# A pre-norm's turn from tokens to channels: rows scaled on VectorE and transposed on TensorE, in place of float32 products with a diagonal matrix

## The chip, the core and the metric

The kernel runs on one core of a Trainium2 chip. The metric is the device time of one execution in microseconds (us), and the changed kernel is compared with the kernel before it on the same chip. Matrix products are done by TensorE (PE in the profile; PEld is its weight load), elementwise work by VectorE (DVE) and ScalarE (ACT), and nearly all weights are loaded by DMAs that SyncE (SP) issues.

## What is computed

A two-layer encoder on 256 tokens of 2048 channels, in float32. Every sub-layer f is, with the shift, scale and gate of an adaLN projection of a conditioning vector c:

```python
x = x + gate * RMSNorm_post(f(RMSNorm_pre(x) * (1 + scale) + shift))

def _rms(x):
    x32 = x.astype(jnp.float32)
    return x32 * lax.rsqrt(jnp.mean(jnp.square(x32), axis=-1, keepdims=True) + EPS)
```

The sub-layers are a convolution module and a gated feed-forward network (layer 0), then gated linear attention and a gated feed-forward network (layer 1). So there are four pre-norms. The change concerns the turn of RMSNorm_pre(x) from rows of tokens to rows of channels, which the products that follow need.

## The kernel before

The residual stream stays on the chip as eight tiles `X[t][c]`: two halves `t` of 128 tokens on the partitions, and four pieces `c` of 512 channels along them. Weights come in blocks of 1 MB (`raw`, DMAs at L95). ScalarE casts a block to a float32r part `hi` (L119), VectorE subtracts to get the rest `lo` (L121), and each product with a weight is done as three float32r products (L751 to L753 in the convolution's first projection `ps_cin`, L406 and L407 in the networks' `ps_fa` and `ps_fb`). The adaLN weights ride along: as rows on VectorE (L348, 128 x 2048) or as columns on TensorE (`ada`, L362), whose sums VectorE turns (`adat`, L369) and TensorE adds (`adas`, L376).

A pre-norm works in three steps. `token_rstd` makes 1/rms of 128 tokens, one number per partition. `token_diag` puts it on the diagonal of a 128 x 128 matrix `dg` (L464). `h_tiles` then takes two blocks of 128 channels at a time and makes, for both halves of the tokens, the product of the block of `X` with `dg` (L474, tile `ps_h`): the product scales the rows and transposes them at once. One `ps_h` tile holds two blocks, so four products. ScalarE writes the modulated norm `h` (L481) and for odd blocks its unrounded copy `hn` (L483), VectorE does `hn` for even blocks (L485) and the part below float32r (L486). In names like `ps_h00_4` the digits are the layer, the norm and the first of the two blocks.

In the convolution's pre-norm the sixteen blocks are made in five steps (blocks 0-1, 2-3, 4-7, 8-11, 12-15), each just behind the adaLN columns of its own scale and shift, between the products of the first projection. The other three pre-norms stand behind a post-norm: `post_norm` adds the sub-layer's output `y` to `X` (L561), sums its squares on ScalarE (L425), keeps TensorE busy meanwhile with products that are not used (`clock`, L549), and calls `token_diag`. There all sixteen blocks follow each other.

Each engine works through its own instructions strictly in the order of a schedule that is made when the program is built; a scheduler lays them out by its own estimates, so a change in one function can move the instructions of others. Temporary tiles come from small pools: `adat`, squares and a few others share three buffers (`sq`).

Of the kernel before, what the change touches and what calls it, by code (L numbers as in the profile page):

```python
# [24 lines left out]
# blocks of channels whose convolution is done on the tensor engine  # L25
PE_BLOCKS = (5, 7, 9, 11, 12, 13, 14, 15)
# blocks whose mean the squares are taken around
NA = 12
# steps of the first projection: input tiles, and the pairs of channels and gates that they meet
STEPS = ((0, 2, 0, 16), (2, 2, 0, 16), (4, 4, 0, 16), (8, 4, 0, 8), (12, 4, 0, 8), (8, 8, 8, 16))  # L30
# adaLN blocks that are loaded after every block of weights of a step
ADA = ((2, 1, 1, 0), (3, 3, 2, 0), (1, 1, 1, 1, 1, 1, 1, 1), (3, 3, 2, 0), (1,) * 4, (1,) * 8)
COLS_CONV = 16
# the heads' steps: a head's waits lie beside the next head's products
# [14 lines left out]
# columns of the packed per-channel parameters  # L49
# [13 lines left out]
class Stream:  # L63
    """Weight blocks in the order they are used: loaded ahead, split into two
    float32r parts ahead of the products; adaLN weights ride along."""

    def __init__(self, tc, ctx, items, ada_row, ada_col, raw_bufs=4, split_bufs=4):
# [15 lines left out]
        # blocks whose parts are kept in another pool  # L83
# [42 lines left out]
    def flush(self):  # L126
        """adaLN products come after the arithmetic that was waiting already."""
        self.finish()
        for it, r in self.late:
            (self.ada_row if it["kind"] == "row" else self.ada_col)(it["key"], r)  # L130
        self.late.clear()

    def finish(self):
        """The sums of products that were taken out of PSUM before."""
        for f in self.sums:
            f()
        self.sums.clear()
# [17 lines left out]
    def prepare(self, n, first=SPLIT_FIRST):  # L155
        """Split the next n blocks."""
        self.first = first
        i = self.pos
        for _ in range(n):
            i = self._next(i) + 1  # L160
        self.run_to(i)
# [15 lines left out]
class Later(list):  # L177
    """Tiles that are made, two at a time, as the first products come to them."""
# [10 lines left out]
def trunk_kernel(ctx: ExitStack, tc: tile.TileContext, x, cvec, ccol, adar, adac, adah, par, taps, wgate,  # L189
# [21 lines left out]
    # per tile of 128 inputs: silu(c) in the first of 32 columns  # L211
# [8 lines left out]
    # channel n of 32 on every partition (i, n)  # L220
# [4 lines left out]
    # the residual stream, tokens on partitions  # L225
# [28 lines left out]
    def ada_step(s):  # L254
        """The adaLN blocks of a step's scale and shift."""
# [89 lines left out]
    def ada_row(key, r):  # L345
        """128 outputs of an adaLN product, rows of the transposed weights."""
# [4 lines left out]
    def ada_col(key, r):  # L351
        """512 outputs of an adaLN product on the tensor engine: four column tiles
        take four input tiles at once, and a product with ones sums their rows."""
# [10 lines left out]
        if i == KT // per - 1:  # L364
            # output 128 c + 32 a + i: four partial sums, on partitions (j, i) of column 32 (4 c + a)
# [29 lines left out]
    pp = {"ps": ctx.enter_context(tc.tile_pool(name="psum", bufs=6, space=PS))}  # L395

    def mm_blocks(keys, act, nk=KT):
        """Columns of 128-wide weight blocks against act (parts hi | lo): PSUM
        [:, :T] + [:, T:] is the product. Several blocks go through the input tiles together."""
# [22 lines left out]
    def token_squares(src, ss, t, c):  # L422
        """The sum of squares of every token over 512 channels."""
# [13 lines left out]
    def warm(func, src):  # L437
        """Brings in a function's table while its data is still on the way."""
# [9 lines left out]
    def add_bias(l, m):  # L448
        """Row products lack their bias; column products have it."""
# [10 lines left out]
    def token_diag(ss, name):  # L460
        """1 / rms of 128 tokens, on the diagonal of a matrix."""
        r = token_rstd(ss, name)
        dg = small.tile([P, P], F32, tag="dgx", name="dgx" + name, bufs=2)
        apool["dg"] = V.tensor_scalar_mul(dg, ident, r)  # L464
        return dg

    def h_tiles(l, which, sh, sc, dg, ks):
        """Channels of the modulated norm: the product with the diagonal scales and transposes."""
        hs = []
        for k0 in ks[::2]:  # L470
            ps = pp["ps"].tile([P, 2, T], F32, tag="ps", name=f"ps_h{l}{which}_{k0}")
            for k in (k0, k0 + 1):
                for t in range(2):
                    nc.tensor.matmul(ps[:, k - k0, t * P : (t + 1) * P], X[t][k // 4][:, (k % 4) * P : (k % 4 + 1) * P],  # L474
                                     dg[t], start=True, stop=True)
# [24 lines left out]
    def gate_rows(l, which, gate, room=None):  # L500
        """gate * norm_g along the channels, the same on every partition."""
# [12 lines left out]
    def token_products(pv, t, parts, act, kt, nk):  # L514
        """A tile of inputs: 512 output channels of half of the tokens."""
# [8 lines left out]
    def mm_tokens(key, act, nk, each, last=False):  # L524
        """512 output channels, tokens on partitions, all the parts summed in PSUM.
        Last: one half of the tokens after the other, so that the first's norm runs
        beside the second's products."""
# [17 lines left out]
    def keep_clock(src, tag="ada"):  # L545
        """Products without a use: the array's clock falls when it waits for long."""
# [4 lines left out]
    def post_norm(l, which, t, ss, ys, last=False):  # L551
        """x += y / rms(y), y with its gains; the sums of squares of the new x."""
# [15 lines left out]
        return None if last else token_diag(sx[t], f"x{l}{which}{t}")  # L568
# [22 lines left out]

    def conv_mixer(l):
        with early as cx:
# [8 lines left out]
            dg = [token_diag(ss[t], f"in{t}") for t in range(2)]  # L602
# [30 lines left out]
            def mean_add(j):  # L633
                """The statistics of the channels: sums, and the squares of the
                distances from the mean of the first NA blocks."""
# [12 lines left out]
            def tap(j, s):  # L648
                """The weights of the channels of a block, s steps back."""
# [3 lines left out]
            def gather(j, ps, last):  # L653
                """The sums over the steps of the inputs of a pair: channels and their gate."""
# [18 lines left out]
            def taps_dve():  # L673
                """The taps of two blocks in turns."""
# [455 lines left out]
```

## The time and the profile before

| | us |
|---|---|
| median of 3 runs | 2391.42 |
| lowest, highest | 2387.24, 2392.43 |
| span of the profiled execution | 2389.3 |
| PE busy in it | 2332.2 |
| DVE busy in it | 1775.8 |
| ACT busy in it | 1226.6 |

The profiled execution is shown with its span from the first to the last instruction; no separate device time is listed for it, and the span lies 2.1 us under the median. Busy time counts an engine's instructions as they lie on the clock, so overlapping ones are counted once. The profile counts each float32 product of `h_tiles` as two matmuls with two weight loads: 256 records for 128 products.

### The profile page before, as it was taken

How to read it: one execution, taken by the hardware profiler on the slowest of the kernel's cores; microseconds unless marked ns; L12 is line 12 of the kernel's file. 1: busy time of each engine (PE TensorE's matmuls, PEld its weight loads, DVE VectorE, ACT ScalarE, POOL GpSimd, SP SyncE). 2: the span in 40 equal slices, each digit the busy share in tenths (PEclk: the TensorE clock that was granted, in tenths of full speed). 3: DMA queues.
4: the chain of work that ended last, by engine and by line, in shares of the span. 5: the costliest groups of instructions: out<-in, count | busy, mean ns of one | idle time of the engine just before them, and what ended most of it. 6: DMA issues, size and time to landing. Idle time of an engine off the chain costs nothing.

```text
span 2389.3 us, 34229 instructions
## 1 busy us (share of the span) xinstructions
PE 2332.2 (98%) x13522; PEld 1952.7 (82%) x13522; DVE 1775.8 (74%) x2522; ACT 1226.6 (51%) x1941; POOL 17.4 (1%) x43
## 2 busy tenths in 40 slices
PE   6999998999999999999999999999999999999998
PEld 5888746788878888888878888887888888888886
DVE  3878998788878888778878876756887466655665
ACT  5334465465534554345565576656554455534543
POOL 0000000000000000000000000000000000000000
PEclk9999998999999999999999999999999999999999
DMA  9877768657799778988947756563777655555553
GB/s 385 363 311 292 303 230 306 258 211 274 291 326 358 286 283 317 365 282 299 339 154 268 282 203 217 176 228 107 290 273 262 214 180 191 185 190 191 192 198 119
DMA packets 86578, 609.31 MB, mean 255 GB/s; under 512 B 10064, under 2 KB 10128, under 8 KB 13456
## 3 DMA queue, kind: packets, MB, share of 16 engines
q1 hardware_dynamic: 84800, 601.84, 68.5%
q0 software_dynamic: 1472, 4.23, 0.6%
q8 instruction: 106, 1.74, 0.3%
q10 hardware_dynamic: 144, 1.05, 0.1%
q14 instruction: 56, 0.46, 0.1%
HBM read 604.94 MB, written 2.13 MB: 254 GB/s over the span
## 4 chain that ended last, share of the span: by engine, by line
PE 94%; DMA 2%; DVE 1%; ACT 1%; issue 0%; SPq 0%; DVEq 0%; ACTq 0%
PE ps_fa L406 13%; PE ps_fb L406 13%; PE ps_fb L407 7%; PE ps_fa L407 7%; PE ps_fo L522 6%; PE ps_fo L521 6%; PE ps_fo L520 6%; PE ps_cin L751 3%; PE ps_cin L752 3%; PE ps_cin L753 3%; PE ps_r L406 3%; PE ada L362 2%; PE ps_r L407 1%; PE ps_cout L520 1%; PE ps_k L406 1%; PE ps_cout L522 1%
## 5 line engine op out<-in xcount | busy, mean ns | idle before, releaser
L121 DVE TENSOR_TENSOR lo<-raw,hi 128x1024 fp32r<-128x1024 f32 (+1 forms) x760 | 914.7, 1214 | 415.3 <-ACT hi L119 412.0
L119 ACT CAST hi<-raw 128x1024 fp32r<-128x1024 f32 (+1 forms) x760 | 784.5, 1042 | 838.3 <-PE ps_fa L406 196.0
L406 PE MATMUL ps_fa<-h,hi 128*128 128x512 f32 x1408 | 501.0, 398 | 0.9 <-ACT h L481 0.9
L406 PE MATMUL ps_fb<-h,hi 128*128 128x512 f32 x1408 | 500.8, 397 | 0.0
L407 PE MATMUL ps_fa<-h,lo 128*128 128x256 f32 x1408 | 394.5, 280 | 1.7 <-DVE lo L121 1.7
L407 PE MATMUL ps_fb<-h,lo 128*128 128x256 f32 x1408 | 394.5, 280 | 1.5 <-DVE lo L121 1.5
L348 DVE CUSTOM_DVE_ANT_0 raw<-raw,cb 128x2048 f32<-128x2048 f32 x140 | 319.8, 2286 | 18.9 <-DMA raw<-in_adar 18.5
L406 PEld LDWEIGHTS ps_fa<-h,hi 128*128 128x128 f32 x1408 | 264.4, 188 | 64.8 <-issue 1.2
L406 PEld LDWEIGHTS ps_fb<-h,hi 128*128 128x128 f32 x1408 | 264.4, 188 | 64.6
L521 PE MATMUL ps_fo<-lo,u 128*128 128x512 f32 x704 | 274.1, 389 | 1.3 <-DVE lo L121 1.3
L522 PE MATMUL ps_fo<-hi,u 128*128 128x512 f32 x704 | 273.9, 389 | 0.0
L520 PE MATMUL ps_fo<-hi,u 128*128 128x512 f32 x704 | 272.8, 389 | 0.0
L407 PEld LDWEIGHTS ps_fa<-h,lo 128*128 128x128 f32 x1408 | 265.7, 189 | 2.8 <-DVE lo L121 2.1
L407 PEld LDWEIGHTS ps_fb<-h,lo 128*128 128x128 f32 x1408 | 265.7, 189 | 1.8 <-DVE lo L121 1.8
L521 PEld LDWEIGHTS ps_fo<-lo,u 128*128 128x128 f32 x704 | 132.2, 188 | 29.4 <-DVE lo L121 2.1
L520 PEld LDWEIGHTS ps_fo<-hi,u 128*128 128x128 f32 x704 | 132.2, 188 | 27.5 <-ACT hi L119 0.2
L522 PEld LDWEIGHTS ps_fo<-hi,u 128*128 128x128 f32 x704 | 132.2, 188 | 27.4
L751 PE MATMUL ps_cin<-h,hi 128*128 128x256 f32 x512 | 147.6, 292 | 6.1 <-ACT hi L119 6.0
L753 PE MATMUL ps_cin<-h,lo 128*128 128x256 f32 x512 | 144.5, 287 | 2.3 <-DVE lo L121 2.3
L752 PE MATMUL ps_cin<-h,hi 128*128 128x256 f32 x512 | 146.2, 288 | 0.4 <-DVE h L486 0.4
L751 PEld LDWEIGHTS ps_cin<-h,hi 128*128 128x128 f32 x512 | 99.6, 196 | 18.3 <-ACT hi L119 8.5
L752 PEld LDWEIGHTS ps_cin<-h,hi 128*128 128x128 f32 x512 | 99.9, 196 | 5.6 <-DVE h L486 4.7
(239 smaller groups left out, 2884.7 us busy)
## 6 DMA issues: line engine op xcount, KB each, us to landing
raw<-in_fin SPq DMA_DIRECT2D x176, 1024.0 KB, 4.8
raw<-in_adar SPq DMA_DIRECT2D x140, 1024.0 KB, 6.1
raw<-in_fout SPq DMA_DIRECT2D x88, 1024.0 KB, 5.0
raw<-in_adac SPq DMA_DIRECT2D x44, 1024.0 KB, 5.5
raw<-in_gin SPq DMA_DIRECT2D x33, 1024.0 KB, 5.7
raw<-in_cin SPq DMA_DIRECT2D x32, 1024.0 KB, 11.3
raw<-in_cout SPq DMA_DIRECT2D x16, 1024.0 KB, 7.0
raw<-in_gv SPq DMA_DIRECT2D x16, 1024.0 KB, 4.8
```

What stands on the lines that cost most here:

```text
L119: nc.scalar.copy(hi[:, :w], r[:, s : s + w])
L121: nc.vector.tensor_sub(lo[:, :w], r[:, s : s + w], hi[:, :w].bitcast(F32))
L348: V.tensor_tensor_reduce(out=r, in0=r, in1=cb, scale=1.0, scalar=0.0, op0=ALU.mult, op1=ALU.add, accum_out=mod[l, m][:, k : k + 1])
L362: nc.tensor.matmul(ps[32 * (j % 4) : 32 * (j % 4) + 32], cz[:, kt], r[:, j * n : (j + 1) * n], start=kt < 4, stop=kt >= KT - 4, tile_posit ...
L406: nc.tensor.matmul(ps, hi(k * P), act[k], start=k == 0, stop=False)
L407: nc.tensor.matmul(ps[:, :T], lo(k * P), act[k][:, :T], start=False, stop=k == nk - 1)
L520: nc.tensor.matmul(pv, ah, wh, start=kt == 0, stop=False)
L521: nc.tensor.matmul(pv, ah, wl, start=False, stop=False)
L522: nc.tensor.matmul(pv, al, wh, start=False, stop=kt == nk - 1)
L751: nc.tensor.matmul(ps[:, b], hi(o), ah, start=k == 0, stop=False)
L752: nc.tensor.matmul(ps[:, b], hi(o), al, start=False, stop=False)
L753: nc.tensor.matmul(ps[:, b], lo(o), ah, start=False, stop=k == nk - 1)
```

## The change

`token_diag` becomes `token_normed`: VectorE multiplies the four 128 x 512 pieces of `X[t]` with 1/rms, into the tiles of the post-norm's `y`, which are no longer needed by then. `h_tiles` transposes the scaled blocks on TensorE. In the convolution's pre-norm, which has no `y` tiles, a function `normed` scales two blocks of one half of the tokens (128 x 256) when they are asked for, into a tile `xs` of the pool's tag `sq`. Line numbers behind these places grow by 1 or 11. Comments and docstrings are dropped too, which changes no instruction.

```diff
-    def token_diag(ss, name):
-        """1 / rms of 128 tokens, on the diagonal of a matrix."""
+    def token_normed(t, ss, xs, name):
         r = token_rstd(ss, name)
-        dg = small.tile([P, P], F32, tag="dgx", name="dgx" + name, bufs=2)
-        apool["dg"] = V.tensor_scalar_mul(dg, ident, r)
-        return dg
+        for c in range(4):
+            i = V.tensor_scalar_mul(xs[c], X[t][c], r)
+            if c == 0:
+                apool["dg"] = i
+        return lambda k: xs[k // 4][:, (k % 4) * P : (k % 4 + 1) * P]
...
                 for t in range(2):
-                    nc.tensor.matmul(ps[:, k - k0, t * P : (t + 1) * P], X[t][k // 4][:, (k % 4) * P : (k % 4 + 1) * P],
-                                     dg[t], start=True, stop=True)
+                    nc.tensor.transpose(ps[:, k - k0, t * P : (t + 1) * P], dg[t](k), ident)
...
-        return None if last else token_diag(sx[t], f"x{l}{which}{t}")
+        return None if last else token_normed(t, sx[t], [ys[t, c] for c in range(4)], f"x{l}{which}{t}")
...
-            dg = [token_diag(ss[t], f"in{t}") for t in range(2)]
+            rs = [token_rstd(ss[t], f"in{t}") for t in range(2)]
+            two = {}
+
+            def normed(t, k):
+
+                if k % 2 == 0:
+                    two[t] = small.tile([P, 2 * P], F32, tag="sq", name=f"xs{t}{k}", bufs=3)
+                    V.tensor_scalar_mul(two[t], X[t][k // 4][:, (k % 4) * P : (k % 4 + 2) * P], rs[t])
+                return two[t][:, k % 2 * P : (k % 2 + 1) * P]
+
+            dg = [lambda k, t=t: normed(t, k) for t in range(2)]
```

The built program has 128 matmuls and 128 weight loads fewer on TensorE, and 32 more multiplications on VectorE. The schedule moves with it, above all in the convolution's first projection. Three places follow, each of before and then of the changed kernel. A row gives the line, the operation, out<-in and the shape.

**Place 1, the step of blocks 4-7.** TensorE before; `ps_cin1_12` is the next product of the projection.

```order
L362 MATMUL ada014_700<-raw21_630,cz_80 32x512 x4
L474 MATMUL ps_h00_4_889<-dgxin0_168,x01_93 128x128
L474 MATMUL ps_h00_4_889<-dgxin1_174,x11_97 128x128
...
L376 MATMUL adas014_877<-adat0140_862,mask32_88 32x2 x4
...
L376 MATMUL adas014_877<-adat014256_864,mask32_88 32x2 x4
L474 MATMUL ps_h00_6_904<-dgxin1_174,x11_97 128x128
L751 MATMUL ps_cin1_12_919<-h00_2_558,hi23_0_794 128x256
```

TensorE in the changed kernel, at the same place:

```order
L362 MATMUL ada014_704<-raw21_634,cz_80 32x512 x4
L376 MATMUL adas014_881<-adat0140_866,mask32_88 32x2 x4
L376 MATMUL adas014_881<-adat014256_868,mask32_88 32x2 x4
L476 MATMUL ps_h00_4_893<-ident_85,xs04_894 128x128
L476 MATMUL ps_h00_4_893<-ident_85,xs14_897 128x128
...
L476 MATMUL ps_h00_6_912<-ident_85,xs06_913 128x128
L762 MATMUL ps_cin1_12_931<-h00_2_562,hi23_0_798 128x256
```

The products with `dg` stood ahead of and between the `adas`; the transposes stand behind both, five of them ahead of the projection's next product. VectorE in the changed kernel there:

```order
L369 STREAM_TRANSPOSE adat0140_866<-ada014_704 128x256
L369 STREAM_TRANSPOSE adat014256_868<-ada014_704 128x256
L121 TENSOR_TENSOR lo23_0_799<-raw23_638,hi23_0_798 128x1024
L121 TENSOR_TENSOR lo23_1024_803<-raw23_638,hi23_1024_802 128x1024
L379 TENSOR_TENSOR m01_101<-adas014_881,pr_84 128x4
L624 TENSOR_TENSOR m00_100<-m00_100,pr_84 128x4
L610 TENSOR_SCALAR xs04_894<-x01_93,trin0_164 128x256
L458 SCALAR_TENSOR_TENSOR m01_101<-m01_101,pr_84 128x4
L610 TENSOR_SCALAR xs14_897<-x11_97,trin1_168 128x256
L610 TENSOR_SCALAR xs06_913<-x01_93,trin0_164 128x256
```

The rows down to L624 stood there before in the same order; the three scalings came in behind them.

**Place 2, the step of blocks 8-11.** VectorE before:

```order
L660 TENSOR_TENSOR pair13_596<-pair13_596,ps_cin2_13_1413 128x512
L348 ISA raw39_1179,m00_100<-raw39_1179,cb_83 128x2048
...
L369 STREAM_TRANSPOSE adat0180_1443<-ada018_1039 128x256
L369 STREAM_TRANSPOSE adat018256_1445<-ada018_1039 128x256
L121 TENSOR_TENSOR lo40_0_1452<-raw40_1242,hi40_0_1451 128x1024
L121 TENSOR_TENSOR lo40_1024_1456<-raw40_1242,hi40_1024_1455 128x1024
```

VectorE in the changed kernel:

```order
L348 ISA raw39_1191,m00_100<-raw39_1191,cb_83 128x2048
...
L671 TENSOR_TENSOR pair13_600<-pair13_600,ps_cin2_13_1425 128x512
L624 TENSOR_TENSOR m00_100<-m00_100,pr_84 128x4
L369 STREAM_TRANSPOSE adat0180_1455<-ada018_1051 128x256
L121 TENSOR_TENSOR lo40_0_1464<-raw40_1254,hi40_0_1463 128x1024
L121 TENSOR_TENSOR lo40_1024_1468<-raw40_1254,hi40_1024_1467 128x1024
L369 STREAM_TRANSPOSE adat018256_1457<-ada018_1051 128x256
L610 TENSOR_SCALAR xs08_1485<-x02_94,trin0_164 128x256
L610 TENSOR_SCALAR xs18_1488<-x12_98,trin1_168 128x256
```

The second `adat` and the scalings came behind the two `lo` of block 40. On TensorE the order is here as at place 1: `ada`, both `adas`, five transposes, and then the next product of the projection; before, all eight products with `dg` and seven products of the projection stood ahead of the first `adas`.

**Place 3, between the steps of blocks 8-11 and 12-15.** VectorE before; `ps_cin3_4` needs `lo48_0`:

```order
L660 TENSOR_TENSOR pair3_346<-pair3_346,ps_cin3_3_1674 128x512
L348 ISA raw47_1449,m00_100<-raw47_1449,cb_83 128x2048
...
L121 TENSOR_TENSOR lo48_0_1641<-raw48_1554,hi48_0_1640 128x1024
L121 TENSOR_TENSOR lo48_1024_1645<-raw48_1554,hi48_1024_1644 128x1024
L660 TENSOR_TENSOR pair4_392<-pair4_392,ps_cin3_4_1720 128x512
L348 ISA raw50_1558,m00_100<-raw50_1558,cb_83 128x2048
...
L660 TENSOR_TENSOR pair5_407<-pair5_407,ps_cin3_5_1746 128x512
```

VectorE in the changed kernel:

```order
L121 TENSOR_TENSOR lo48_0_1661<-raw48_1574,hi48_0_1660 128x1024
L121 TENSOR_TENSOR lo48_1024_1665<-raw48_1574,hi48_1024_1664 128x1024
L671 TENSOR_TENSOR pair3_346<-pair3_346,ps_cin3_3_1694 128x512
L348 ISA raw47_1461,m00_100<-raw47_1461,cb_83 128x2048
...
L671 TENSOR_TENSOR pair4_392<-pair4_392,ps_cin3_4_1740 128x512
L671 TENSOR_TENSOR pair5_407<-pair5_407,ps_cin3_5_1766 128x512
L348 ISA raw50_1578,m00_100<-raw50_1578,cb_83 128x2048
```

The two `lo` of block 48 moved ahead of the row sum of block 47, and `pair5` moved ahead of the row sum of block 50. Behind it follow the step's two `adat` and its scalings; before, the `adat` stood there too.

In the other three pre-norms the order changes little: four multiplications of 128 x 512 stand on VectorE where one `dg` stood (for `t` = 0 ahead of the last piece of the post-norm's `t` = 1, for `t` = 1 ahead of a `lo` and the first `hn`), and half as many rows on TensorE where the products with `dg` stood. Outside the pre-norms and the first 350 us the order is the same.

## Rows read from the trace of the kernel before

**Rows 1.** The page: busy time, share and instructions by engine; the ending chain.

```profile
PE 2332.2 (98%) x13522; PEld 1952.7 (82%) x13522; DVE 1775.8 (74%) x2522; ACT 1226.6 (51%) x1941; POOL 17.4 (1%) x43
...
PE 94%; DMA 2%; DVE 1%; ACT 1%; issue 0%; SPq 0%; DVEq 0%; ACTq 0%
```

**Rows 2.** Groups by shape: busy us, mean ns of one, idle before and releaser.

```profile
L474 PE MATMUL ps_h<-dgxx,x 128*128 128x128 f32 x192 | 26.2, 274 | 0.0
L485 DVE TENSOR_SCALAR hn<-ps_h,m,m 128x256 f32<-128x256 f32 x32 | 17.4, 543 | 6.3 <-ACT h L481 5.7
L844 DVE TENSOR_TENSOR yf<-yf,g 128x512 f32<-128x512 f32 x16 | 10.7, 687 | 3.9 <-ACT junk L425 2.9 <-ACT warm L440 1.0
```

**Rows 3.** The one 128 x 256 SBUF product with constants: minimum/median/maximum ns, start.

```profile
L643 DVE TENSOR_SCALAR part_a<-mean_a x1: 294/294/294, 328.4 to 328.4; 128x256 f32<-128x256 f32 x1
```

**Rows 4.** Timeline of TensorE, step of blocks 4-7: start us, duration us, instruction.

```profile
84.73 1.38 PE L474 MATMUL ps_h<-dgxin,x 128*128 128x128 f32 x10
...
87.27 0.36 PE L751 MATMUL ps_cin<-h,hi 128*128 128x256 f32 x1
```

**Rows 5.** Timeline of VectorE, the same step.

```profile
85.10 0.77 DVE L369 STREAM_TRANSPOSE adat<-ada 128x256 f32<-128x256 f32 x2
85.79 2.32 DVE L121 TENSOR_TENSOR lo<-raw,hi 128x1024 fp32r<-128x1024 f32 x2
```

**Rows 6.** Timeline of TensorE, step of blocks 8-11.

```profile
138.21 1.06 PE L362 MATMUL ada<-raw,cz 128*32 128x512 f32 x8
139.21 2.05 PE L474 MATMUL ps_h<-dgxin,x 128*128 128x128 f32 x16
```

**Rows 7.** Timeline of VectorE, the same step.

```profile
138.92 2.29 DVE L348 CUSTOM_DVE_ANT_0 raw<-raw,cb 128x2048 f32<-128x2048 f32 x1
141.13 0.78 DVE L369 STREAM_TRANSPOSE adat<-ada 128x256 f32<-128x256 f32 x2
141.83 2.32 DVE L121 TENSOR_TENSOR lo<-raw,hi 128x1024 fp32r<-128x1024 f32 x2
```

**Rows 8.** Timeline of VectorE at place 3 and the step of blocks 12-15.

```profile
164.02 2.28 DVE L348 CUSTOM_DVE_ANT_0 raw<-raw,cb 128x2048 f32<-128x2048 f32 x1
...
166.23 2.36 DVE L121 TENSOR_TENSOR lo<-raw,hi 128x1024 fp32r<-128x1024 f32 x2
...
172.54 2.28 DVE L348 CUSTOM_DVE_ANT_0 raw<-raw,cb 128x2048 f32<-128x2048 f32 x1
```

**Rows 9.** Timeline of TensorE, the same stretch.

```profile
167.50 0.39 PE L753 MATMUL ps_cin<-h,lo 128*128 128x256 f32 x1 [2.32 <-DVE lo L121]
...
174.46 1.06 PE L362 MATMUL ada<-raw,cz 128*32 128x512 f32 x8
...
177.31 0.94 PE L474 MATMUL ps_h<-dgxin,x 128*128 128x128 f32 x6
```

**Rows 10.** TensorE by windows: stretch, its us, busy us, granted clock, DMA share, GB/s.

```profile
168.00:172.00 4.00, 4.00 (x24) 0.57 1.01 426
```

**Rows 11.** Waits, 80 to 200 us: total us, times, longest.

```profile
PEld ps_cin L752 <- DVE h L486: 4.7, 5, 1.3
```

**Rows 12.** Waits of the DMA queue, 80 to 200 us: total us, times, longest.

```profile
SPq L95 <- PE ada L362: 62.5, 9, 11.8
```

**Rows 13.** Timeline of VectorE ahead of the post-norms' last pieces, idle time in brackets.

```profile
463.79 0.69 DVE L579 TENSOR_TENSOR y<-ps_cout,gs 128x512 f32<-128x512 f32 x1 [0.94 <-PE ps_cout L522]
...
1221.06 0.69 DVE L844 TENSOR_TENSOR yf<-yf,g 128x512 f32<-128x512 f32 x1 [0.45 <-ACT junk L425]
...
1626.74 0.69 DVE L579 TENSOR_TENSOR y<-ps_gout,g 128x512 f32<-128x512 f32 x1 [2.27 <-PE ps_gout L522]
```

**Rows 14.** Timeline of TensorE at the first network's pre-norm.

```profile
473.57 2.17 PE L474 MATMUL ps_h<-dgxx,x 128*128 128x128 f32 x18
```

**Rows 15.** Timeline of ScalarE there: the first tile of two successive pairs.

```profile
474.44 0.56 ACT L481 ACTIVATE h<-ps_h,m,m 128x256 fp32r<-128x256 f32 x1 [3.55 <-PE ps_h L474]
...
476.53 0.56 ACT L481 ACTIVATE h<-ps_h,m,m 128x256 fp32r<-128x256 f32 x1
```

## The prediction

> **What bounds the kernel now.** I read the page first: TensorE is busy for 98% of the span and makes up 94% of the chain that ended last [rows 1]. So what TensorE no longer does comes back unless a wait takes its place, and every wait put on TensorE costs its whole length. Then I read the groups by shape for prices, and the timelines of the pre-norms for who is late there. In the convolution's first projection the weights don't run ahead far enough to swallow a delay either: the queue that issues the DMAs waited nine times, 62.5 us in all, for TensorE to be done with an adaLN block [rows 12], so a late TensorE makes the next loads late too. I add delays of TensorE up to the end.
>
> **What is removed.** 18 records of the old products begin and end within 2.17 us, and one lasts 0.274 us by itself [rows 2, 14]: (2.17 - 0.27) / 17 = 0.112 us for each. A product with `dg` is two records, a transpose one. If a transpose costs what one such record costs, 128 x 0.112 = 14.3 us of TensorE's time go, 3.6 us in each norm. No row shows a transpose. It can't save more than the whole product (0.224 us), and where its mode is slow it saves nothing; I take 0.112, the price of a record with the same 128 columns of weights.
>
> **What is added on VectorE.** A 128 x 256 multiplication between SBUF tiles by constants took 0.294 us [rows 3], the same shape out of PSUM 0.543 [rows 2]. `xs` lies in SBUF, so I take 0.30 and keep 0.54 as the upper end. For 128 x 512 the bounds are 0.294 (half the columns) and 0.687 (two tensors) [rows 2, 3]; I take the middle, 0.49, 1.96 us for four. The `dg` that goes has fewer columns than the 0.294 row; at 0.29 for it, a half of the tokens costs 1.67 us more.
>
> **The three later norms.** ScalarE and VectorE need 476.53 - 474.44 = 2.09 us for a pair of `h` tiles [rows 15], while TensorE needed some 2.17 for a pair: 8 records (0.89) and the 1.28 us of products with it, which is my estimate from the spacing. Taking 0.45 off TensorE makes the pair's time 2.09, not 1.72: the arithmetic behind `ps_h` binds. What comes back is 0.08 for each of seven pairs, and 0.45 because the first tile needs four records and not eight: 1.0 us in a norm, 3.0 in three. Against it stand the multiplications for the first half of the tokens, ahead of the last piece of the post-norm. VectorE was idle there for 0.94, 0.45 and 2.27 us [rows 13], so 1.67 us more leaves 0.7, 1.2 and 0 us. Those for the second half delay only the first `hn`, behind the `clock` products; the 1.0 above absorbs that. Net -1.1 us.
>
> **The convolution's norm** has the larger terms, by the order at the three places shown.
>
> Blocks 4-7: TensorE had the old products to do while VectorE turned `adat`, from 84.73, and its next product began at 87.27 [rows 4]. Now it waits for `xs`, and all its later products are queued behind. VectorE ends `adat` at 85.87, the two `lo` at 88.11 [rows 5], two small sums take 0.16, and three scalings with one small operation between them end at 89.1. The fifth transpose ends at 89.2, 1.95 us later than before, and three more come among the next products (0.33): +2.3.
>
> Blocks 8-11: the second `adat` now stands behind two `lo`. `ada` ends at 139.2, the first `adat` can follow at 139.3, then come `lo` twice (2.32), the second `adat` (0.36) and two scalings, until 143.0 [rows 6, 7]. TensorE resumes at about 143.4, and loses another 0.3 on the last transposes, where the old products ended at 141.1 and two `adas` (0.34) came later: +2.4. This holds if the row sum L348, which ran from 138.92 [rows 7], comes earlier, since what stood ahead of it now stands behind it. If it ends when it did, the wait is 1.9 us longer.
>
> Place 3: before, `lo` of block 48 stood behind a row sum that ran from 164.02, and TensorE waited 2.32 us for it until 167.50 [rows 8, 9]. Now it stands ahead: -2.3. Right behind that wait the clock was granted at 0.57 for 4 us [rows 10], the lower of its two levels (1.2 and 2.4 GHz) for most of them. Against the full clock that is 0.43 x 4 = 1.7 us, which go as well: -4.0.
>
> Blocks 12-15: before, TensorE went from the start of `ada` at 174.46 to the next product of the projection at 178.0 (six records from 177.31), 3.5 us [rows 9]. Now `pair5` waits for the product ahead of `ada`, then come the row sum (2.28 [rows 8]), `adat` and the scalings: 0.7 + 2.3 + 0.7 + 1.2, and 0.2 for transposes that are left: 5.1. So +1.6.
>
> The two steps ahead of these have short waits of the same kind, `xs` behind `adat` (0.4 and 0.2 by the multiplications' price): +0.6. Part of it all is swallowed: five times TensorE waited for the lower part of `h`, its weight loader for 4.7 us in all [rows 11]; the loader waits longer than the array, and I take half, -2.4.
>
> **The clock.** The wait of 2.32 us was followed by the lower clock. TensorE now has three waits of about 2.5 to 3.5 us, with only short `adas` between. I take the fall behind each at its price in the row: 3 x 1.7 = +5.1.
>
> Sum: 0.6 + 2.3 + 2.4 - 4.0 + 1.6 - 2.4 + 5.1 - 1.1 = +4.5 us. On the span of 2389.3 that is 2393.8. The span lies 2.1 us under the median of 2391.42, and on the median it is 2395.9, rounded to 2396. 0.2% is 4.8 us, about what a measurement of this kernel can tell from no change, so the forecast lies at that bound.
>
> **Rivals.**
>
> *TensorE's saving comes back* (faster). If the arithmetic behind `ps_h` doesn't hold up the norms, they give 3 x 3.6 = 10.8 and not 3.0 us; with no fall of the clock the convolution costs 5.1 less. The first alone gives 2396 - 7.8 = 2388, both 2383. For it: TensorE's share of the chain [rows 1]. Against it: the steady 2.09 us [rows 15]. It decides if a pair takes under about 1.9 us. Chance 0.17. The Trainium skill (Perfetto Trace Analysis, "Transposes") wants a logical transpose done as a transpose and not as a matmul, which would point here; no row of this kernel shows a transpose.
>
> *The clock doesn't fall, or the stalls are shorter* (no change). Without the 5.1 us it is 2391. For it: the `adas` and transposes lie within the waits. Chance 0.2.
>
> *Transposes are slow* (slower). At 0.224 us, the price of the product, all 128 save nothing: the norms lose the 3.0 us, and the convolution loses 32 x 0.112 = 3.6 that the steps' terms counted: 2402.5. From 0.16 on it shows. For it: nothing in the rows, as no row shows a transpose; the two engines that wait behind them would show it in each norm. Chance 0.13. The Trainium skill ("TensorE: Matmul & The Clock Gate", Part 4: PE-mode transpose) speaks for it: it gives about 275 ns for a transpose in a kernel, and says that the full clock doesn't engage for this mode. By that figure I estimate 128 x (0.275 - 0.224) = 6.5 us more than the product's price, some 2409; no run here shows it yet.
>
> *VectorE's scalings are dear* (slower). At 0.54 the eight scalings that TensorE waits for cost 8 x 0.24 = 1.9 more, and with 0.687 for the long ones the first halves' covers are overrun by 3 x 0.8 = 2.4 more: 2400. It decides from about 0.35 and 0.55. Chance 0.12.
>
> **How the numbers follow.** The forecast has 0.38, with a range of its own from 2391.5 to 2401 (the wait at blocks 8-11 1.9 us longer, one fall more or less, the `h` waits' 2.4 gained or not). Half of it lies over the bound: 0.22 slower, 0.16 same. The slow cases add 0.25. No fall gives same 0.18 and faster 0.02; the faster case splits, 0.14 faster and 0.03 same. Faster 0.16, same 0.37, slower 0.47. The range goes from 2385, inside the faster case, to 2405, past the slower ones without the skill's figure.
>
> **What would show it.** In the changed trace: `ps_h` records one for each transpose, about 0.11 us apart; VectorE's `xs` near 0.30 and the 128 x 512 ones near 0.49; TensorE waiting for `xs` at about 86 us and for `adas` near 140, each followed by a stretch at the lower clock; no wait for `lo` near 165; pairs of `h` 2.09 us apart in the networks' norms, with TensorE now waiting for `h`. I am wrong if TensorE never waits for `xs`, if the clock stays full behind those waits, or if a pair of `h` takes as long as TensorE's own work.

## The result and the profile after

| | before | changed |
|---|---|---|
| median, us (4 runs each, on the same chip) | 2389.61 | 2401.74 |
| lowest to highest, us | 2387.24 to 2392.43 | 2399.41 to 2402.93 |
| span of the profiled execution, us | 2389.3 | 2398.9 |

The changed kernel is slower: the ratio is 1.0047, with an interval from 1.0034 to 1.0060, or +11 us (8 to 14). The two profiled executions differ by 9.6 us, and it is these 9.6 that the rows can account for.

The page of the changed kernel, busy time by engine and the ending chain, answers to [rows 1]:

```profile
PE 2324.2 (97%) x13394; PEld 1938.7 (81%) x13394; DVE 1787.2 (74%) x2554; ACT 1227.5 (51%) x1941; POOL 17.4 (1%) x43
...
PE 92%; DVE 3%; DMA 2%; ACT 2%; issue 1%; SPq 0%; DVEq 0%; ACTq 0%
```

TensorE has 128 matmuls fewer and is busy 8.0 us less, yet the span is longer. Its share of the chain fell from 94% to 92%, and VectorE's rose from 1% to 3%: TensorE now waits for VectorE. The new operations, in the groups by shape (busy us, mean ns of one, idle before and releaser), answer to [rows 2, 3]:

```profile
L476 PE MATMUL ps_h<-ident,y 128*128 128x128 f32 x64 | 10.6, 272 | 0.0
L476 PE MATMUL ps_h<-ident,xs 128*128 128x128 f32 x32 | 7.3, 352 | 2.8 <-DVE m L458 2.5 <-PE adas L376 0.2
L464 DVE TENSOR_SCALAR y<-x,trx 128x512 f32<-128x512 f32 x16 | 6.7, 482 | 0.2
L610 DVE TENSOR_SCALAR xs<-x,trin 128x256 f32<-128x256 f32 x16 | 5.1, 341 | 2.2 <-PE ps_h L476 2.2
```

A transpose is one record. The `xs` transposes have a mean of 352 ns against 272, although the shape is the same; the windows below say why. The last row has a wait that tells of the buffers: `xs` needs only `X` and 1/rms, so where it waited 2.2 us for `ps_h` it had no free buffer until the transposes had read an earlier `xs`.

Waits of TensorE between 20 and 200 us, most first (total us, times, longest; other rows of the view are left out):

```profile
PE adas L376 <- DVE adat L369: 7.8, 7, 2.4
...
PE ps_h L476 <- DVE m L458: 2.5, 1, 2.5
```

Before, the waits for `adat` in the same stretch came to 1.1 us in all. The wait of `ps_h` is put down to `m` (L458), but what it needs is the scaling `xs`, which stands right beside that small operation. The timeline of TensorE at the three steps (start us, duration us, instruction, idle time in brackets) answers to [rows 4, 6, 9]:

```profile
87.96 0.57 PE L376 MATMUL adas<-adat,mask 128*32 128x2 f32 x16 [0.80 <-DVE adat L369]
91.03 1.36 PE L476 MATMUL ps_h<-ident,xs 128*128 128x128 f32 x5 [2.50 <-DVE m L458]
92.04 0.56 PE L762 MATMUL ps_cin<-h,hi 128*128 128x256 f32 x1
...
144.12 1.07 PE L362 MATMUL ada<-raw,cz 128*32 128x512 f32 x8
...
148.37 0.28 PE L376 MATMUL adas<-adat,mask 128*32 128x2 f32 x8 [2.36 <-DVE adat L369]
...
150.32 1.33 PE L476 MATMUL ps_h<-ident,xs 128*128 128x128 f32 x5
...
179.43 1.07 PE L362 MATMUL ada<-raw,cz 128*32 128x512 f32 x8
...
182.86 0.57 PE L376 MATMUL adas<-adat,mask 128*32 128x2 f32 x16 [2.36 <-DVE adat L369]
```

VectorE at the first of the three answers to [rows 5]:

```profile
87.46 0.77 DVE L369 STREAM_TRANSPOSE adat<-ada 128x256 f32<-128x256 f32 x2
88.16 2.32 DVE L121 TENSOR_TENSOR lo<-raw,hi 128x1024 fp32r<-128x1024 f32 x2
...
90.54 0.35 DVE L610 TENSOR_SCALAR xs<-x,trin 128x256 f32<-128x256 f32 x1
```

The step's `ada` ended at 87.1, and VectorE had `adat` done by 88.23. Then came two `lo`, 2.32 us, which TensorE read only behind the transposes (the first product with a `lo` starts at 92.62), and only then the scalings. TensorE waited for the first two of them with all of its projection behind the transposes. The windows of TensorE (stretch, its us, busy us, granted clock, DMA share, GB/s), first at the first projection products and then at two of the steps, answer to [rows 10]:

```profile
32.00:36.00 4.00, 4.00 (x24) 0.63 1.01 420
...
90.00:92.00 2.00, 0.97 (x5) 0.50 1.00 422
92.00:94.00 2.00, 2.00 (x11) 0.50 1.06 446
...
96.00:98.00 2.00, 2.00 (x18) 0.90 1.04 438
...
152.00:154.00 2.00, 2.00 (x11) 0.50 0.70 295
```

A clock of 0.50 is the lower of the two levels: 11 records in 2 us where the kernel before had 14 to 19 between 88 and 98 us at 1.00. Most `xs` transposes of these steps run in such stretches, which fits the 352 ns that one of them takes.

**Where the 9.6 us are.** The start of the last `clock` group of the post-norm behind the convolution moved from 467.52 to 475.49 us: +8.0. From there to the first network's first product it is 8.67 us before and 9.71 after, +1.0. In the other two norms, from the first `clock` product of the post-norm to the first product that needs `h`, it is 11.07 and then 12.34 (+1.3), and 11.03 and then 11.48 (+0.45). The work between the norms gave back 0.3 to 0.55 in each stretch, 1.1 in all. 8.0 + 1.0 + 1.3 + 0.45 - 1.1 = 9.6.

### The profile page after: what moved, and what is told of

Its sections match the earlier page's. It is cut to its first block, busy times and chain, and to the rows that moved or that the text cites. A ratio compares the mean times of both kernels' runs of the same rounds, so it can differ in the third digit from the quotient of the medians.

```text
span 2398.9 us, 34027 instructions
## 1 busy us (share of the span) xinstructions
PE 2324.2 (97%) x13394; PEld 1938.7 (81%) x13394; DVE 1787.2 (74%) x2554; ACT 1227.5 (51%) x1941; POOL 17.4 (1%) x43
## 4 chain that ended last, share of the span: by engine, by line
PE 92%; DVE 3%; DMA 2%; ACT 2%; issue 1%; SPq 0%; DVEq 0%; ACTq 0%
PE ps_fa L406 13%; PE ps_fb L406 13%; PE ps_fb L407 7%; PE ps_fa L407 7%; PE ps_fo L522 6%; PE ps_fo L523 6%; PE ps_fo L521 6%; PE ps_cin L762 3%; PE ps_cin L764 3%; PE ps_cin L763 3%; PE ps_r L406 3%; PE ada L362 2%; PE ps_r L407 1%; PE ps_k L406 1%; PE ps_gout L523 1%; PE ps_v L521 1%
## 5 line engine op out<-in xcount | busy, mean ns | idle before, releaser
L762 PE MATMUL ps_cin<-h,hi 128*128 128x256 f32 x512 | 151.1, 296 | 4.4 <-ACT hi L119 4.4
L763 PE MATMUL ps_cin<-h,hi 128*128 128x256 f32 x512 | 147.9, 290 | 0.0
L762 PEld LDWEIGHTS ps_cin<-h,hi 128*128 128x128 f32 x512 | 102.0, 199 | 18.6 <-ACT hi L119 8.9
L764 PEld LDWEIGHTS ps_cin<-h,lo 128*128 128x128 f32 x512 | 101.3, 199 | 3.3 <-issue 1.7
```

The costliest lines, as they stand in the source:

```text
L762: nc.tensor.matmul(ps[:, b], hi(o), ah, start=k == 0, stop=False)
L763: nc.tensor.matmul(ps[:, b], hi(o), al, start=False, stop=False)
L764: nc.tensor.matmul(ps[:, b], lo(o), ah, start=False, stop=k == nk - 1)
```

## The experiments

My theory after the result: the transposes are as cheap as forecast, but the scalings put VectorE on TensorE's path: in the convolution because they come late (their buffers are shared with `adat`), each wait with a fall of the clock behind it; in the later norms because four of them stand ahead of the first `hn`. Rivals: the transposes themselves are slow or hold the clock down; the shift of all later work, not the clock, is the price. Ratios are to the kernel before on the same chip, with 95% intervals. Profiles are single executions: from the first network's first product to the next post-norm they need between 742.6 and 748.3 us in the kernels that scale all later norms ahead, and between 741.4 and 747.0 in those with the later norms of before. So totals are compared by ratios and places by rows.

**One half of the change at a time.** `later_only` makes the convolution's norm as before:

```diff
-            rs = [token_rstd(ss[t], f"in{t}") for t in range(2)]
...
-            dg = [lambda k, t=t: normed(t, k) for t in range(2)]
+            dg = [token_diag(ss[t], f"in{t}") for t in range(2)]
```

> The convolution's pre-norm is as before the change (diagonal matrices), the other three pre-norms as in the changed kernel. Theory (the loss lies in the convolution's steps, where transposes wait for late scalings and the clock falls behind the waits; the two traces' milestones put 7.6 us there and 2.0 us in the other three norms): about 2391.6 us against 2389.6 before. Rival (the transposes themselves are dear, by their mode or by the clock that they don't hold): 96 of the 128 transposes stay, so three quarters of the loss of 12 us, about 2398.7.

`conv_only` makes the other three as before:

```diff
-        return None if last else token_normed(t, sx[t], [ys[t, c] for c in range(4)], f"x{l}{which}{t}")
+        return None if last else token_diag(sx[t], f"x{l}{which}{t}")
```

> The convolution's pre-norm is as in the changed kernel, the other three as before it. Theory (late scalings in the convolution's steps): about 2397 us, three quarters of the loss. Rival (the transposes themselves): 32 of 128, a quarter of the loss, about 2392.6.

`later_only` measured 1.0018 (1.0009 to 1.0028) and `conv_only` 1.0029 (1.0016 to 1.0042). Both halves lose, and the two losses add up to the whole, 0.0047. So the three later norms, which I had put down as a gain of 1.1 us, lose about 4 (2 to 7 by the interval). The rows above give them only 2.0, and from `bufs_conv_only` to `conv_bufs`, below, it is 2.6: the direction is shown, the size is between these.

**Transposes without the scaling.** `no_scale` transposes the rows of `X` as they are, so 1/rms is left out of all four norms; VectorE writes the small `dg` again, which no one reads. The cut shows the later norms; the convolution's is changed likewise.

```diff
-            i = V.tensor_scalar_mul(xs[c], X[t][c], r)
...
-        return lambda k: xs[k // 4][:, (k % 4) * P : (k % 4 + 1) * P]
+        return lambda k: X[t][k // 4][:, (k % 4) * P : (k % 4 + 1) * P]
```

> All four pre-norms transpose the rows of X themselves, so that 1/rms is left out of them: the same 128 transposes, none of the scalings. Theory (the loss comes from waiting for the scalings): TensorE keeps 3.6 us of the convolution's norm and about 1 us of each other norm, so about 2383 us (2379 to 2387), with no wait at the steps. Rival (transposes are slow, or the clock falls by them): 2394 or more, and low clock behind the transposes without a wait ahead of them.

It measured 0.9972 (0.9960 to 0.9983), 2382.95 us, -6.3 us. The timeline of TensorE in it at the step of blocks 4-7, and then its windows over that step and the two after it:

```profile
84.45 1.06 PE L362 MATMUL ada<-raw,cz 128*32 128x512 f32 x8
85.45 1.09 PE L474 MATMUL ps_h<-ident,x 128*128 128x128 f32 x8
86.47 0.24 PE L376 MATMUL adas<-adat,mask 128*32 128x2 f32 x8
```

```profile
84.00:90.00 6.00, 6.00 (x62) 1.00 1.00 425
138.00:144.00 6.00, 6.00 (x62) 1.00 0.63 214
...
174.00:180.00 6.00, 6.00 (x61) 1.00 1.02 426
```

Eight transposes begin and end within 1.09 us. With 0.28 for the last (the group's mean is 281 ns) that is 0.81 / 7 = 0.116 us for each, and TensorE never waits in these stretches nor loses its clock. So the transposes aren't the loss; what they save is there once no scaling stands ahead of them. Part of the 6.3 us is the clock, though: from 28 to 32 us and from 168 to 172 us it is at 1.00 in this execution, where the kernel before has 0.57. A record lasts some 275 ns, which is just the figure that the Trainium skill ("TensorE: Matmul & The Clock Gate", Part 4: PE-mode transpose) gives for a bf16 one in a kernel; the rows show that this is how long one takes, not how far apart they are. The same section of the Trainium skill also says that the full clock doesn't engage for transposes. Here it stays at 1.00 through eight of them; whether it would through a long run of nothing else no run shows.

**Scaled rows, products instead of transposes.** `products` keeps the scalings and all else:

```diff
-                    nc.tensor.transpose(ps[:, k - k0, t * P : (t + 1) * P], dg[t](k), ident)
+                    nc.tensor.matmul(ps[:, k - k0, t * P : (t + 1) * P], dg[t](k), ident, start=True, stop=True)
```

> The changed kernel with its scalings, but float32 products of the scaled rows with the identity in place of the transposes (two records for one). It prices the half of the change that was to gain. Theory (a transpose saves one 0.11 us record, which counts in the convolution and at the norms' first tile only): 2 to 6 us more than the changed kernel, about 2405. Rival (transposes are no gain, since they hold no clock): 2401.7 or less.

It measured 1.0047 (1.0035 to 1.0059), as the changed kernel did. I had expected 2 to 6 us more. Once VectorE scales the rows, twice as many records on TensorE cost nothing that can be measured, which is to some 4 us. It does not follow that they are free: with them the clock falls less at the steps than in the changed kernel. Its windows behind the waits of the first two steps:

```profile
96.00:102.00 6.00, 6.00 (x41) 0.72 1.02 429
...
148.00:154.00 6.00, 3.50 (x37) 1.00 0.98 403
```

From the `ada` of blocks 4-7 to the end of the projection's products `products` needs 186.3 us and the changed kernel 189.2, after it had started that step 3.6 us later. What the records cost by themselves, without the clock, is not shown. The Trainium skill (Perfetto Trace Analysis, "Transposes") asks for a transpose in place of a matmul; the records are indeed half as many here, and the time is the same.

**Buffers of their own.** In `conv_bufs` only the tile `xs` changes its pool and tag, so `adat` no longer waits for the buffers of `xs`, nor `xs` for those of `adat`:

```diff
-                    two[t] = small.tile([P, 2 * P], F32, tag="sq", name=f"xs{t}{k}", bufs=3)
+                    two[t] = cm.tile([P, 2 * P], F32, tag="xs", name=f"xs{t}{k}", bufs=3)
```

> The changed kernel with one edit: the scaled tiles xs of the convolution get three buffers of their own in place of the three shared with adat and the squares. The built order then has the transposes ahead of the adas again. Theory, sharper (the scalings are late because their buffers wait for adat's): most of the convolution's 7.6 us comes back, about 2393 us (2390 to 2396). Rival (VectorE has no time for sixteen more multiplications, wherever they stand): 2399 or more.

`bufs_conv_only` has the same edit with two buffers, and the other three norms as before:

> The convolution's norm scaled and transposed with two buffers of its own for xs, the other three norms with the diagonal matrix as before the change. Theory (the other norms lose 2.0 us by their scalings): 2389.9 - 2.0 = 2387.9 (2386 to 2390), a little faster than before the change. Rival (with two buffers the scalings wait again): 2393 or more.

`conv_bufs` measured 1.0004 (0.9994 to 1.0014) and `bufs_conv_only` 0.9993 (0.9983 to 1.0004). The tag alone brings back nearly the whole loss, a little more than I had expected (2389.89 us, against 2390 to 2396). It also moves later tiles in the memory, but the pace of the projection's products stays at 0.120 us, so that isn't what it changes. The scheduler now puts the scalings ahead of the step, as TensorE's timeline of `conv_bufs` at blocks 4-7 shows, and its waits between 20 and 200 us below it:

```profile
85.31 1.07 PE L362 MATMUL ada<-raw,cz 128*32 128x512 f32 x8
86.31 0.76 PE L476 MATMUL ps_h<-ident,xs 128*128 128x128 f32 x5
87.17 0.24 PE L376 MATMUL adas<-adat,mask 128*32 128x2 f32 x8
87.35 0.38 PE L762 MATMUL ps_cin<-h,hi 128*128 128x256 f32 x1
```

```profile
PE adas L376 <- DVE adat L369: 1.2, 2, 0.6
```

The transposes stand where the products with `dg` stood, between `ada` and `adas`, and cover VectorE's turn of `adat`. From the end of `ada` to the projection's next product it is 1.0 us; in the changed kernel it was 4.9. With the order of before the wait for `lo` at place 3 is back too, 2.17 us until 168.20, so what the changed kernel gained there is no part of this. With two buffers (`bufs_conv_only`) it is the other way round: a wait of 2.50 us for the scalings at blocks 4-7 and the fall behind it are there again, the wait at place 3 is not, and the convolution's last products end within 0.5 us of those in `conv_bufs`.

**The clock alone.** `filled` is the changed kernel with two products that no one uses in the waits of the three steps; the rest of the order is the same:

```diff
+            if l == 0 and which == 0 and k0 in (4, 8, 12):
+                for _ in range(2):
+                    nc.tensor.matmul(ps.rearrange("p a b -> p (a b)"), ident, X[0][0], start=True, stop=True)
```

> The changed kernel with two unused float32 products of 128x512 (four records, about 1.7 us) ahead of the transposes in the convolution's steps of blocks 4, 8 and 12, so that TensorE works inside its waits; the built order is otherwise the same. It tells the wait from the clock's fall behind it. Theory (each wait costs its length and then 1.7 us by the lower clock): the waits stay, the falls go, 2401.7 - 3 x 1.7 = about 2396.6 (2394 to 2399). Rival (only the waits cost, the low clock lies beside VectorE's work anyway): 2401 to 2402. Rival (the transposes themselves pull the clock down): the falls stay, 2401 or more.

It measured 1.0018 (1.0009 to 1.0028). The windows of TensorE at the same steps:

```profile
84.00:90.00 6.00, 5.13 (x45) 1.00 1.01 425
90.00:96.00 6.00, 5.24 (x42) 1.00 1.01 429
...
148.00:154.00 6.00, 6.00 (x51) 1.00 0.78 296
...
184.00:190.00 6.00, 6.00 (x52) 1.00 1.01 425
```

TensorE still waits for VectorE (0.9 and 0.8 us idle in the first two stretches, the fillers beside), but the clock stays full. From the start of one step's `ada` to that of the next the filled kernel needs 2.2 us less than the changed one over blocks 4-7 and 2.5 less over blocks 8-11 and place 3; from there to the end of the projection's products it is 1.1 less. The last of these products in the kernel before, the changed and the filled kernel, from three timelines:

```profile
267.15 0.28 PE L753 MATMUL ps_cin<-h,lo 128*128 128x256 f32 x1
274.99 0.28 PE L764 MATMUL ps_cin<-h,lo 128*128 128x256 f32 x1
268.97 0.28 PE L767 MATMUL ps_cin<-h,lo 128*128 128x256 f32 x1
```

From the `ada` of blocks 4-7 to that end it is 183.7 us before, 189.2 in the changed and 183.3 in the filled kernel. So the three falls cost 5.8 us, and the waits themselves, with what place 3 gave back, nothing. Behind the projection the filled kernel loses 1.5 us again, so that the convolution's last group of products ends only 4.5 us earlier than in the changed kernel: TensorE waits there for a DMA, 12.41 us before, and in the changed and the filled kernel

```profile
375.58 1.93 PE L362 MATMUL ada<-raw,cz 128*32 128x512 f32 x8 [13.64 <-DMA raw<-in_adac]
370.41 1.94 PE L362 MATMUL ada<-raw,cz 128*32 128x512 f32 x8 [14.44 <-DMA raw<-in_adac]
```

with the clock lower for longer behind it in the filled kernel. By the ratios (1.0047 and 1.0018) the falls are 6.9 us, with an interval that holds 5.8. The span of this profiled execution, 2399.1 us, shows no gain, because it needed 748.3 us for the first network, where the changed kernel's needed 742.6.

**Scaling as the tiles come.** In the later norms `later_lazy` and `bufs_lazy` scale only the first piece of 512 channels ahead, and each other piece when its blocks are near. The first has the convolution's norm as before, the second the buffers of `conv_bufs`. Their 1/rms also got a tag of its own, `trx`:

```diff
-        r = token_rstd(ss, name)
-        for c in range(4):
-            i = V.tensor_scalar_mul(xs[c], X[t][c], r)
+        r = token_rstd(ss, name, "trx")
...
+        def scaled(k):
+            for c in {k // 4, min((k + 2) // 4, 3)} - done:
+                i = V.tensor_scalar_mul(xs[c], X[t][c], r)
```

> The convolution's norm with diagonal matrices as before the change; the other three norms scaled and transposed, with only the first 128x512 piece of the second half of the tokens scaled ahead of the h tiles. The same norms with all four pieces ahead took 1.0018 of the time before. Theory (about 1.3 us in each norm is the first hn's wait behind four scalings): 1.0000 to 1.0010. Rival (the scalings cost the same wherever they stand, since VectorE and ScalarE are the norms' bound): 1.0018.

> Scaled and transposed in all four norms, xs with three buffers of its own; in the other three norms only the first 128x512 piece of the second half of the tokens is scaled ahead of the h tiles, the other three as the tiles come to them. Theory (the first hn waits on VectorE behind four scalings, about 1.3 us in each norm): 2389.9 - 2 to 3 = about 2387.5 (2385.5 to 2389.5). Rival (the chain of ScalarE and VectorE takes the same time wherever the scalings stand): 2389.9.

`bufs_lazy_b` is the same kernel as `bufs_lazy` once more, on another chip:

> The fastest full version so far once more (own buffers for xs, pieces of the second half scaled as the tiles come to them), to tell whether it beats the kernel before: 0.9992 with an interval that reached 1.0000 the first time. Expected 0.9985 to 1.0000; at 1.0000 or more it is no gain.

`later_lazy` measured 1.0002 (0.9993 to 1.0012) against 1.0018 of `later_only`. `bufs_lazy` measured 0.9992 (0.9983 to 1.0000), and again 0.9978 (0.9969 to 0.9987): the only version with scalings that was ever faster than the kernel before, clearly in one comparison and at the edge in the other. What the edit does shows at the last pre-norm. VectorE and TensorE there in the changed kernel:

```profile
1643.60 1.68 DVE L464 TENSOR_SCALAR y<-x,trx 128x512 f32<-128x512 f32 x4
1645.19 1.22 DVE L121 TENSOR_TENSOR lo<-raw,hi 128x1024 fp32r<-128x1024 f32 x1
1646.32 0.54 DVE L486 TENSOR_SCALAR hn<-ps_h,m,m 128x256 f32<-128x256 f32 x1
```

```profile
1644.40 1.15 PE L476 MATMUL ps_h<-ident,y 128*128 128x128 f32 x9
1647.47 0.47 PE L406 MATMUL ps_fa<-h,hi 128*128 128x512 f32 x1 [1.92 <-ACT h L482]
```

and TensorE in `bufs_lazy`:

```profile
1632.43 0.82 PE L483 MATMUL ps_h<-ident,y 128*128 128x128 f32 x6
1634.56 0.55 PE L483 MATMUL ps_h<-ident,y 128*128 128x128 f32 x3 [1.30 <-DVE y L467]
1634.98 0.47 PE L406 MATMUL ps_fa<-h,hi 128*128 128x512 f32 x1
```

and before:

```profile
1634.95 2.17 PE L474 MATMUL ps_h<-dgxx,x 128*128 128x128 f32 x18
1637.57 0.47 PE L406 MATMUL ps_fa<-h,hi 128*128 128x512 f32 x1 [0.45 <-ACT h L481]
```

From the first transpose to the first product it is 3.07 us in the changed kernel, 2.55 in `bufs_lazy` and 2.62 before. In the attention's norm, from the first `clock` product to the first product, it is 12.34, 11.37 and 11.07.

**The tag alone.** Since the tag also moves later tiles by a few bytes, two kernels change only that: `before_trx` in the kernel before, `bufs_trx` in `conv_bufs`. The order of both is that of the kernel they come from, on every engine.

```diff
-        r = token_rstd(ss, name)
+        r = token_rstd(ss, name, "trx")
```

> The kernel before the change, with 1/rms of its later norms in a pool tag of its own: two more tiles of 4 bytes on each partition, no instruction added, and the same order on every engine. Only the places of the tiles behind them move. In the two kernels that have this tag the first projection's products came 0.114 us apart and not 0.120. Theory (the place of the operands sets that spacing, not the change): the 0.114 us here too, and 0.998 to 0.9995 of the time before. Rival (the lazy scalings made the gain): no difference, 0.9995 to 1.0005.

> The changed kernel with own buffers for xs, all pieces scaled ahead, and the same tag of its own for 1/rms. Theory (the tag's place makes most of the gain of the version that scales pieces as the tiles come): 0.998 to 0.9995 of the time before, close to that version's 0.9978 and 0.9992. Rival (scaling the pieces late makes the gain): 1.0004, as without the tag.

`before_trx` measured 1.0003 (0.9993 to 1.0013) and `bufs_trx` 0.9998 (0.9989 to 1.0007). I had expected the tag to make the gain, and it doesn't: it changes no total that can be measured, so the step from 1.0018 to 1.0002 isn't its doing by itself. But from `bufs_trx` to `bufs_lazy` only the lazy scaling is new, and 0.9998 against 0.9992 and 0.9978 puts its worth anywhere between nothing and 0.2%. The rows show that the 0.5 and 1.0 us come back at two norms, and that the lazy scaling does it (in `bufs_trx` the attention's norm takes 12.34 us, as in the changed kernel); how much of it reaches the end stays open.

## Why the prediction was right, and where its sizes were off

The direction and the range were right, and so was the mechanism in the convolution; two terms of the sum were mis-sized, both too low. The measured 2401.74 us lies just above the forecast's own range (2391.5 to 2401). That the stated range holds it is in part luck: two slow rivals had widened it, and neither came true.

- **Prices.** A transpose at 0.112 us: nine take 1.15 us, less 0.27 for the last, 0.11 each. A scaling at 0.30 and 0.49: 0.341 and 0.482. A pair of `h` at 2.09: the tiles start at 1646.90, 1648.99 and 1651.08 us. All held. The rivals of slow transposes and dear scalings fall with them.
- **Blocks 4 to 15 and place 3.** From the end of `ada` of one step to that of the next, the changed kernel needs 3.5 us more over blocks 4-7 (taken: 2.3, and 1.7 for the clock, less the step's part of what is swallowed), 0.9 less over blocks 8-11 and place 3 together (taken: 2.4 + 1.7 - 4.0, less its part; the 2.4 is 2.3 by its own figures), and 2.6 more from there to the convolution's last products (taken: 1.6 + 1.7). No wait for `lo` is left near 165 us. With the first two steps the convolution's last products come 7.6 us later, where the terms came to 5.6. The clock fell behind all three waits. `filled` gives 5.8 us for the three falls (2.2, 2.5 and 1.1, where I had taken 1.7 for each), and -0.4 us for all the rest of these steps, where the terms without the clock come to -0.1. No wait of the weight loader for `h` is left between 80 and 200 us, so the 2.4 us put down as swallowed fit too.
- **The first two steps were mis-sized: +0.6 taken, +2.4 measured** (the `ada` of blocks 4-7 starts at 86.09 us, before at 83.73). I priced the scalings and forgot the clock: it was at 0.57 from 28 to 32 us before and back at 1.00 from 32; now TensorE waits longer in that stretch and it is at 0.63 until 36 us, with 24 records in those 4 us instead of 35. But this size isn't firm, and that the scalings made it isn't shown: in `before_trx` and `later_lazy`, whose convolution norm has no scalings, the clock is at 0.50 from 28 to 32 us and at 0.79 and 0.72 in the next 4.
- **The later norms were mis-sized: -1.1 taken, +2.0 measured.** The step that failed is "the 1.0 above absorbs that". ScalarE does get its first tile sooner, 0.53 us after the first transpose, where it was 0.87 [rows 14, 15]. But the first `hn` stands on VectorE behind the four scalings and a `lo`, 1.92 us after the first transpose instead of 1.47, and the first product needs it: TensorE waits 1.92 us for `h`, where it waited 0.45. The pairs then go at ScalarE's and VectorE's 2.09 us, so nothing makes up for it but 0.3 to 0.55 us in each stretch that follows. In the attention's norm the multiplication ahead of the last piece is late as well (the `clock` products for `t` = 1 start 0.8 us later), and in the first network's the `clock` products take 7.59 us instead of 6.22, at the lower clock. That last size is not firm: behind the same wait of 1.86 us the group took 4.65 us in `conv_bufs` and `before_trx` and 7.49 in `later_only`.
- **TensorE's saving comes back** was the rival on the other side. It does if the scaling is left out (-6.3 us in `no_scale`), so TensorE's load was worth something, but the scaling can't be had for nothing on the path where it stands.

That the shared buffers set the order in the convolution was not in the prediction. The order at place 2 showed the second `adat` behind two `lo`; I took it as given, and didn't ask what in the change had made it. `conv_bufs` shows it.

## What to carry to other kernels

Work moved from the bounding engine to one with spare time pays only if the new work is done before it is asked for: compare where the helper's instruction stands with where the bounding engine needs it, not the two busy times. A temporary tile that joins a pool in use becomes a tie between the two uses, and a scheduler then moves both; give it buffers of its own before judging the change (here 1.0047 went to 1.0004). Price a wait on TensorE with the stretch at the lower clock that may follow it: behind the three here it cost 1.1 to 2.5 us, and without it the projection lost nothing from blocks 4-7 on.

## What the hardware showed that I had not expected

Two tiles of 4 bytes per partition more (the tag `trx`), with the same order of every instruction, change the pace of the float32r products. The windows of TensorE for the kernel before:

```profile
100.00:130.00 30.00, 30.00 (x249) 1.00 0.85 343
```

and for `before_trx`:

```profile
100.00:130.00 30.00, 30.00 (x262) 1.00 0.91 365
```

The products of the convolution's first projection come every 0.115 us instead of 0.120, at the same clock, and the first network's first product starts at 468.49 us instead of 476.19. Part of these 7.7 us is given back: from the attention's first `ps_q` product to the next post-norm it takes 397.9 us instead of 395.7, in the other four executions with the tag 397.5 to 399.3, and in all without it 395.3 to 397.0. Another 2.7 us go in the first network's stretch, which differs by more than that between executions of one order. In these two executions 2.6 us are left at the end, but by the ratio the totals are the same (1.0003). The edit changes nothing but where later tiles lie in the memory and which buffer holds 1/rms, so I take the place as the cause; which tile matters wasn't tried.

And a wait is not always followed by the lower clock. In `no_scale` TensorE waited for the same `lo` as at place 3 before; its timeline and its window behind that:

```profile
167.48 0.38 PE L755 MATMUL ps_cin<-h,lo 128*128 128x256 f32 x1 [2.46 <-DVE lo L121]
```

```profile
168.00:172.00 4.00, 4.00 (x35) 1.00 1.01 428
```

After 2.46 us of waiting the clock is 1.00, where after 2.32 us it was 0.57 [rows 9, 10]; ahead of both it was 1.00 and TensorE fully busy. What decides between the two wasn't found.
